# The second part of the modulation starts beside the context's products, from a spare buffer and spare PSUM banks, at low priority

## The chip, the cores and the metric

One core of one Trainium2 chip runs the whole layer in one launch. The metric is the device time of one execution in microseconds (us); lower is better. Before and after are compared by the median of several executions on the same chip.

## What is computed

One layer of a diffusion backbone over 1024 latent tokens of width 1024, with 256 context tokens. Cut to what matters:

```
mod(c)      = silu(c) @ w_mod + b_mod          # six parts of 1024: sh1 sc1 gt1 sh2 sc2 gt2
hx, hc      = rms_norm(x or ctx) * (1 + sc1) + sh1
s_f, s_b    = delta-rule states of the context (k, v, gates from hc @ w_in)
p           = hx @ w_in                        # q, k, v, z, gates, pool channels
y           = concat(delta rule(p) started from s_f, s_b ; grid pooling(p)) @ w_out
x           = x + gt1 * rms_norm(y)
x           = x + gt2 * rms_norm(conv_glu_ffn(rms_norm(x) * (1 + sc2) + sh2))
```

The modulation falls in two parts. The first (sh1 and sc1, for the latent and the context) is needed before any product with `w_in`. The second (gt1, sh2, sc2, gt2: 4096 columns of `w_mod`, 16.8 MB in float32) is needed only behind the output projection.

## The kernel before, in words

All products with large weights are made in three float32r products of a high and a low part (`hi*hi`, `lo*hi`, `hi*lo`), so every weight is split first: a rounding copy on ScalarE (ACT) and a subtraction on VectorE (DVE) or GpSimd (POOL).

The order of the work is not written out. `Streams` (lines 128 to 174) is a planner: every stage is a generator with a priority number (low goes first), and at each step the ready generator of the lowest number issues its next few instructions. What is ready when comes from `Clock` (lines 48 to 109), which keeps a planned time for each engine, a cost for each instruction and a planned landing time for each DMA. A generator yields the tiles, the named events (`"PP"`, `"X4"`, `"hX0"`) or the counted buffers (`("s", 1)`) that it waits for. All loads here are issued by `dma = SY.dma_start`, so they share SyncE's (SP's) queue. The profile's order within an engine follows this plan closely, but not to the letter.

The stages that matter here, with their priorities:

- `stream_mod` (0, line 328): the first part of the modulation, 16 loads of 512 KB. At its twelfth (`i + NW == 16`, line 355) it issues the loads of `POST` (line 34: the first context weight, latent tiles 4 to 7, four more context weights) and signals `X4`.
- `stream_xT`, `stream_h`, `stream_x1` (0 to 3): norms, transposes and the modulated `h_hi`, `h_lo` of the context and of both halves of the latent tokens ("X0", "X1"), each followed by 16 gate products (`gate_mm`, line 411, in a bank of `pc`).
- `stream_load` (3, line 546) and `stream_G` (9, line 1269): 28 jobs of large products. Jobs 0 to 7 are the context's (24 products of 256 columns each, results `pa<-c_hi,w_hi` and the like); jobs 8 to 27 are the latent's (48 products of 512 columns each, `pa<-h_hi,w_hi`). At job 8, when `hX0` and `hX1` are there, `open_gemm` (line 657) closes the pool of the loads, opens the pool `pp` and signals `PP`.
- `stream_A` (2), `stream_P` (1), `stream_Q` (0): preparation, triangular solve and scan of the delta rule, head by head. `stream_G` has the highest number, so its products fill what the others leave of TensorE (PE).
- `mod_rest` (line 1231, priority 1, spawned at line 1857): the second part of the modulation, in 32 pieces. It waits for `PP`. A piece loads two halves of 256 KB (`w_m2` in `pp`, shown as `w_m<-in_wmod`), makes eight products of 128 columns with `cs` (which the profile counts as 16, `pb<-w_m,cs`), copies the result to `mrow` on ACT, transposes it on PE (`pb<-cst,mrow`) and sums four columns on ACT (`mjk`). It has two halves of weights in all, so a piece's loads go into the buffers of the piece before. After the last piece it makes the tables `a2`, `ggd` and signals `M`, and `stream_wo(1)` takes over its buffers.
- `stream_W`, `stream_wt` and the feed-forward stages behind them, from about 580 us to the end.

PSUM has eight banks: `pa` 2, `pb` 2, `pc` 4. `slot` (line 282) hands out 4 KB buffers: before `open_dn` there are four, of which `kc`, `vc` and `gx` take three; the count `"s"` says how many are free. `cp` (line 274) is the pool of the context, closed by `open_dn`.

Of the kernel before, what the change touches and what calls it, by code (L numbers as in the profile page):

```python
# [9 lines left out]
F32 = mybir.dt.float32  # L10
# [7 lines left out]
P = 128  # L18
# [109 lines left out]
class Streams:  # L128
# [7 lines left out]
    def spawn(self, gen, prio):  # L136
        self.active.append([prio, max(self.now, self.clock.end), gen, None, 0])

    def signal(self, name):
        self.events[name] = max(self.now, self.clock.end)  # L140

    def free(self, kind, n):
        self.left[kind] = self.left.get(kind, 0) + n
        self.freed[kind] = max(self.now, self.clock.end)
# [38 lines left out]
def kernel(ctx: ExitStack, tc: tile.TileContext, I, out):  # L183
# [4 lines left out]
    streams = Streams(clock)  # L188
    spawn, signal, free = streams.spawn, streams.signal, streams.free
    dma = SY.dma_start  # L190
# [58 lines left out]
    def pb(shape):  # L249
        return psB.tile(shape, F32, name="pb", tag="pb")  # L250
# [23 lines left out]
    cp = cctx.enter_context(tc.tile_pool(name="hc", bufs=1, side="left", reuse_waits="tile"))  # L274
# [7 lines left out]
    def slot(name):  # L282

        kind = "k" if slots["k"] else "big"
        slots[kind] -= 1
        x = (da if kind == "k" else dp).tile([P, T], F32, name=name, tag=kind, bufs=NK if kind == "k" else NBIG)
        slot_of[x.name] = kind
        return x

    def free_slots(*xs):  # L290
        for x in xs:
            slots[slot_of[x.name]] += 1
        free("s", len(xs))
# [237 lines left out]
    def stream_gx():  # L531
        yield "gX0"
        yield "gX1"
        yield "Tc"
        yield from gate_tables("x", NT, gx, gtmp)
        free_slots(gx)
# [9 lines left out]
    def stream_load():  # L546
        ws = {}

        def load(i, m):
            c, h = jobs[i]  # L550
            j = h if c == "c" else {0: 4, 2: 8, 1: 0, 3: 12, 4: 16}[c] + h
            ws[i, m] = wp.tile([P, 4, P], F32, name="w_st", tag="w_st", bufs=2)
            dma(out=ws[i, m], in_=I["w_in_t"][j][:, 4 * m:4 * m + 4])

        for i in range(len(jobs)):
            his, los = [], []
            if i == 0:
                yield "w0"
            if i == 1:
                yield "X4"  # L560
                for j in range(NW):
                    if j not in wcs:
                        load_c(j)
            if i < NCJ:
                for m in range(2):
                    ws[i, m] = wcs[i][:, 4 * m:4 * m + 4]
            if i > 1:
                yield f"J{i - 2}"
            if i == NCJ - 1:
                load(NCJ, 0)  # L570
                load(NCJ, 1)
            for m in range(2):
                w = ws[i, m]
                yield (w,)
                whi = wp.tile([P, 4, P], F32R, name="w_hi", tag="w_hi")
                wlo = wp.tile([P, 4, P], F32R, name="w_lo", tag="w_lo")
                yield from split_steps(whi, wlo, w, *(SPLITS[m] if i < NCJ else (V,)))
                his.append(whi)
                los.append(wlo)
                if NCJ <= i < len(jobs) - 1:  # L580
                    load(i + 1, m)
            if i + NW < NCJ:
                load_c(i + NW)
            win[i] = his, los
            yield (whi, wlo)
            signal(f"L{i}")
        free("st0", 2)
        spawn(stream_wo(0), 5)
        spawn(mix_load(), 2)
# [637 lines left out]


    def mod_rest():
        yield "PP"  # L1230
        for j in range(32):
            ws = []
            for m in range(2):
                ws.append(pp.tile([P, 4, P], F32, name="w_m2", tag="w_m2", bufs=2))
                dma(out=ws[m], in_=I["wmod2"][j, :, 4 * m:4 * m + 4, :])
            yield tuple(ws)
            ps = pb([P, P])
            for k in range(KT):
                g = 32 * (k % 4)
                TE.matmul(ps[g:g + 32, :], lhsT=cs[:, k, :], rhs=ws[k // 4][:, k % 4, :], start=(k < 4), stop=(k >= 4),  # L1240
                          skip_group_check=True)
            yield (ps,)
            rows = pp.tile([P, P], F32, name="mrow", bufs=1)
            S.copy(rows, ps)
            yield (rows,)
            mp = pb([P, P])
            TE.transpose(mp, rows, ident)
            yield (mp,)
            jk = small.tile([P, 4], F32, name="mjk")
            S.activation(jk, mp[:, 0:P:32], AF.Copy, accum_out=mod[:, 16 + j, 0:1])  # L1250
            yield
        V.tensor_tensor(mod[:, 16:48, 0], mod[:, 16:48, 0], bm[:, 16:48], ALU.add)
        V.scalar_tensor_tensor(a2, mod[:, 32:40, 0], 1.0, sm[:, SM_GPREF:SM_GPREF + 8], ALU.add, ALU.mult)
        ggc = small.tile([P, 2, 8], F32, name="ggc")
        V.tensor_tensor(ggc[:, 0], mod[:, 16:24, 0], sm[:, SM_GPOST:SM_GPOST + 8], ALU.mult)
        V.tensor_tensor(ggc[:, 1], mod[:, 40:48, 0], sm[:, SM_GPOSTF:SM_GPOSTF + 8], ALU.mult)
        yield
        gp = pb([P, P])
        TE.transpose(gp[:16, :], ggc.rearrange("p a k -> p (a k)"), ident)
        ggs = pp.tile([P, P], F32, name="mrow", bufs=1)[:16]  # L1260
        S.copy(ggs, gp[:16, :])
        dma(out=ggd.rearrange("a k p -> (a k) p"), in_=ggs)
        yield
        signal("M")
        free("st1", 2)
        spawn(stream_wo(1), 5)
# [45 lines left out]
    def stream_wo(g):  # L1312

        pool, tag = ((wp, "w_st"), (pp, "w_m2"))[g]
        gs = slice(512 * g, 512 * g + 512)
        ks = (4, 5, 6, 7, 0, 1, 2, 3)
        ws = []

        def load():
            ws.append(pool.tile([P, 4, P], F32, name="wo_st", tag=tag, bufs=2).rearrange("p k n -> p (k n)"))  # L1320
            dma(out=ws[-1], in_=I["w_out"][ks[len(ws) - 1] * P:(ks[len(ws) - 1] + 1) * P, gs])

        for i, k in enumerate(ks):
            while len(ws) < min(i + 2, KT):
                yield f"st{g}", 1
                load()
            yield f"U{k}"
            yield (ws[i],)
            if k not in wo:
                wo[k] = [hslot(f"wo_{x}{k}") for x in "hl"]  # L1330
            yield from split_steps(wo[k][0][:, gs], wo[k][1][:, gs], ws[i])
            free(f"st{g}", 1)
            signal(f"WO{g}{k}")
        signal(f"WO{g}")
# [519 lines left out]
    spawn(stream_P(), 1)  # L1854
    spawn(stream_A(), 2)
    spawn(stream_gx(), 1)
    spawn(mod_rest(), 1)
    spawn(stream_load(), 3)
    spawn(stream_G(), 9)
    spawn(stream_wt(), 2)  # L1860
# [81 lines left out]
```

## Time and profile before

| | us |
|---|---|
| median of 3 runs | 1380.78 |
| the three runs | 1374.93, 1380.78, 1381.83 |
| the profiled execution: its own time | 1374.41 |
| its span in the profile | 1372.7 |
| PE busy in the span | 1276.5 (93%) |

The span runs from the first to the last instruction of the profile; 1.71 us lie around it. PE is TensorE's matmul stream, whose busy time counts the whole latency of a product, so that products in close order overlap. A row of the timeline gives start, duration, engine, operation, result and operands, count, and in brackets the idle time before it with what ended it. SPq is SyncE's queue of DMA issues.

### The profile page before, as it was taken

The page shows a single profiled execution, that of the slowest core. Times are in us where ns is not written, and L with a number is a line of the kernel's source. Part 1 is how long each engine was busy: PE and PEld are TensorE (multiplying, and loading weights), DVE is VectorE, ACT ScalarE, POOL GpSimd, SP SyncE. Part 2 cuts the span into 40 slices and gives each one's busy share as a digit, 9 for nine tenths or more (in the row PEclk, how much of TensorE's full clock was granted, in tenths as well). Part 3 has the DMA queues.
Part 4 walks back from the last instruction along what each step waited for, and adds up shares of the span by engine and source line. Part 5 has one row for each costly group of instructions (what it writes and reads, how often), then busy time and mean ns, then how long its engine had stood idle before and what let it go on. Part 6 is the DMA issues. An engine that isn't in the chain of part 4 may idle for free. (4 is left out here: it accounts for less than half of the span.)

```text
span 1372.7 us, 23957 instructions
## 1 busy us (share of the span) xinstructions
PE 1276.5 (93%) x8655; PEld 1003.6 (73%) x8655; DVE 999.7 (73%) x2027; ACT 624.3 (45%) x1478; POOL 333.8 (24%) x431
## 2 busy tenths in 40 slices
PE   5888999999999799988979999999999999999997
PEld 1456767777878678766767777787788887888886
DVE  1876655656788688459888998888887769655674
ACT  3555866456676345345443332332333236644540
POOL 0552434141131500012023323332333220000122
PEclk9889999999999999999999999999999999999999
DMA  9513655445462313483224465566433337976561
GB/s 344 193 41 111 204 175 146 141 131 186 120 197 70 101 58 94 151 268 136 110 74 140 166 237 210 213 230 230 154 138 123 116 122 257 308 251 197 187 212 62
DMA packets 145302, 226.55 MB, mean 165 GB/s; under 512 B 53440, under 2 KB 66592, under 8 KB 142368
## 3 DMA queue, kind: packets, MB, share of 16 engines
q1 hardware_dynamic: 144752, 224.61, 48.4%
q8 instruction: 68, 1.11, 0.3%
q14 instruction: 50, 0.41, 0.1%
q10 hardware_dynamic: 432, 0.42, 0.1%
HBM read 164.77 MB, written 60.21 MB: 164 GB/s over the span
## 5 line engine op out<-in xcount | busy, mean ns | idle before, releaser
L123 POOL TENSOR_TENSOR a<-a,a 128x512 f32<-128x512 f32 x88 | 137.9, 1568 | 354.2 <-DMA a<-in_w_up_t 130.1
L123 ACT CAST wqh<-a 128x512 fp32r<-128x512 f32 x132 | 81.1, 620 | 238.9 <-POOL a L123 62.1
L123 DVE TENSOR_TENSOR op<-dst,op 128x512 fp32r<-128x512 f32 x154 | 104.1, 717 | 62.2 <-ACT op L123 61.9
L123 PE MATMUL pa<-h_hi,w_hi 128*128 128x512 f32 x320 | 138.2, 432 | 2.5 <-ACT jk L123 1.2
L123 ACT CAST op<-dst 128x512 fp32r<-128x512 f32 x154 | 89.8, 620 | 99.1 <-PE pc L123 34.2
L123 PE MATMUL pa<-h_hi,w_lo 128*128 128x512 f32 x320 | 129.6, 405 | 1.6 <-DVE w_lo L123 1.6
L123 PE MATMUL pa<-h_lo,w_hi 128*128 128x512 f32 x320 | 130.5, 408 | 0.0
L123 PE MATMUL pc<-op 128*128 128x512 f32 x528 | 121.7, 391 | 1.3 <-DVE graw L123 1.3
L123 PEld LDWEIGHTS pc<-op 128*128 128x128 f32 x528 | 99.1, 188 | 23.2 <-DVE graw L123 1.7
L123 DVE TENSOR_TENSOR wql<-a,wqh 128x512 fp32r<-128x512 f32 x132 | 101.3, 769 | 19.0 <-ACT wqh L123 18.6
L123 DVE TENSOR_TENSOR hf<-hf 128x512 f32<-128x512 f32 x89 | 82.4, 933 | 2.2 <-DMA hf<-in_w_down 1.7
L123 POOL TENSOR_TENSOR hf<-hf,gg 128x512 f32<-128x512 f32 x16 | 21.2, 1350 | 213.7 <-ACT t L123 213.7
L123 PEld LDWEIGHTS pa<-h_hi,w_hi 128*128 128x128 f32 x320 | 61.1, 191 | 16.0 <-issue 2.8
L123 PEld LDWEIGHTS pa<-h_hi,w_lo 128*128 128x128 f32 x320 | 60.9, 190 | 13.9 <-DVE w_lo L123 1.8
L123 DVE SCALAR_TENSOR_TENSOR cv<-raw,sm,cv 128x1024 f32<-128x1024 f32 x48 | 62.3, 1297 | 11.4 <-ACT cv L123 10.9
L123 PEld LDWEIGHTS pa<-h_lo,w_hi 128*128 128x128 f32 x320 | 61.1, 191 | 9.5 <-issue 2.0
L123 DVE SCALAR_TENSOR_TENSOR hf<-graw,sm,hf 128x1024 f32<-128x1024 f32 x44 | 58.5, 1330 | 0.5
L123 PE MATMUL pa<-op 128*128 128x512 f32 x198 | 50.6, 391 | 0.0
L123 PE MATMUL pb<-op 128*128 128x512 f32 x198 | 50.4, 390 | 0.0
L123 ACT ACTIVATE ws<-pc,btg 128x128 f32<-128x128 f32 x80 | 26.9, 367 | 48.6 <-PE pc L123 48.3
L123 DVE TENSOR_TENSOR w_lo<-w_st,w_hi 128x512 fp32r<-128x512 f32 x40 | 27.6, 692 | 26.7 <-ACT w_hi L123 16.9
L123 PE MATMUL pc<-wo_h,mxh 128*128 128x512 f32 x112 | 44.4, 398 | 1.4 <-ACT mxh L123 1.4
(384 smaller groups left out, 3350.1 us busy)
## 6 DMA issues: line engine op xcount, KB each, us to landing
a<-in_w_up_t SPq DMA_DIRECT2D x90, 256.0 KB, 2.7
w_m<-in_wmod SPq DMA_DIRECT2D x64, 256.0 KB, 3.2
hf<-in_w_down SPq DMA_DIRECT2D x22, 512.0 KB, 4.2
td<-hf SPq DMA_DIRECT2D x11, 1024.0 KB, 4.5
gd<-hf SPq DMA_DIRECT2D x22, 512.0 KB, 2.8
sd<-hf SPq DMA_DIRECT2D x11, 1024.0 KB, 3.9
dst<-sd SPq DMA_DIRECT2D x44, 256.0 KB, 5.2
dst<-td SPq DMA_DIRECT2D x44, 256.0 KB, 4.8
```

The lines of the kernel that those rows point to most:

```text
L123: return f(*a, **k)
```

## The change

`mod_rest` starts at `X4` instead of `PP`, with priority 7 instead of 1. It takes the fourth 4 KB buffer (`wmk`) as its two halves of weights until `PP` is signalled, and then goes over to `w_m2` in `pp` and gives the buffer back. Until then its two PSUM tiles of a piece come from `pc` instead of `pb`, and its row of results stands in a new 512-byte tile of the context's pool. The loads of the next piece are now issued inside the piece: the first half right behind the fourth product, the second right behind the eighth; before, both were issued when the whole piece was done.

```diff
     def mod_rest():
-        yield "PP"
+        yield "X4"
+        yield "s", 1
+        wk = slot("wmk")
+        early = [wk[:, 512 * m:512 * m + 512].rearrange("p (k n) -> p k n", n=P) for m in range(2)]
+        mrow = cp.tile([P, P], F32, name="mrow0")
+
+        def load(j, m):
+
+            if j < 32:
+                first = m == 0 and "PP" not in streams.events or m == 1 and src[j, 0] is early[0]
+                src[j, m] = early[m] if first else pp.tile([P, 4, P], F32, name="w_m2", tag="w_m2", bufs=2)
+                dma(out=src[j, m], in_=I["wmod2"][j, :, 4 * m:4 * m + 4, :])
+
+        src = {}
+        load(0, 0)
+        load(0, 1)
         for j in range(32):
-            ws = []
-            for m in range(2):
-                ws.append(pp.tile([P, 4, P], F32, name="w_m2", tag="w_m2", bufs=2))
-                dma(out=ws[m], in_=I["wmod2"][j, :, 4 * m:4 * m + 4, :])
-            yield tuple(ws)
-            ps = pb([P, P])
+            ws = src[j, 0], src[j, 1]
+            if wk is not None and ws[0] is not early[0]:
+                free_slots(wk)
+                wk = None
+            pool = pb if wk is None else pc
+            yield ws
+            ps = pool([P, P])
             for k in range(KT):
                 g = 32 * (k % 4)
                 TE.matmul(ps[g:g + 32, :], lhsT=cs[:, k, :], rhs=ws[k // 4][:, k % 4, :], start=(k < 4), stop=(k >= 4),
                           skip_group_check=True)
+                if k == 3:
+                    load(j + 1, 0)
+            load(j + 1, 1)
             yield (ps,)
-            rows = pp.tile([P, P], F32, name="mrow", bufs=1)
+            rows = mrow if wk is not None else pp.tile([P, P], F32, name="mrow", bufs=1)
             S.copy(rows, ps)
             yield (rows,)
-            mp = pb([P, P])
+            mp = pool([P, P])
             TE.transpose(mp, rows, ident)
             yield (mp,)
...
-    spawn(mod_rest(), 1)
+    spawn(mod_rest(), 7)
```

## Rows read from the trace of the kernel before

**Rows 1.** Stretches: us, PE, PEld, DVE, ACT, POOL busy, PE clock, DMA share, GB/s

```profile
111.00:200.00 89.00, 80.40 (x882) 58.76 (x882) 52.03 (x138) 61.13 (x187) 25.70 (x45) 0.94 0.58 179
...
300.00:350.00 50.00, 44.14 (x737) 35.23 (x736) 32.42 (x113) 30.11 (x108) 8.83 (x22) 0.97 0.49 152
...
450.00:500.00 50.00, 40.81 (x610) 32.54 (x610) 38.24 (x119) 20.43 (x64) 19.06 (x45) 0.93 0.30 85
```

**Rows 2.** The same view, the stage of the context's products

```profile
40.00:50.00 10.00, 9.60 (x57) 5.41 (x53) 6.69 (x11) 5.25 (x12) 3.57 (x3) 0.91 0.12 47
50.00:60.00 10.00, 8.79 (x74) 4.96 (x72) 9.36 (x16) 8.13 (x19) 6.57 (x6) 1.00 0.94 368
60.00:70.00 10.00, 5.36 (x27) 2.83 (x27) 10.00 (x26) 4.64 (x10) 5.91 (x4) 0.95 0.28 96
70.00:80.00 10.00, 8.57 (x34) 5.11 (x35) 8.43 (x27) 3.70 (x11) 8.35 (x7) 0.53 0.03 11
80.00:90.00 10.00, 7.76 (x56) 6.08 (x54) 8.06 (x13) 6.27 (x11) 6.43 (x6) 1.00 0.01 2
90.00:100.00 10.00, 8.54 (x53) 3.57 (x53) 7.56 (x11) 4.67 (x8) 5.47 (x4) 1.00 0.18 62
```

**Rows 3.** Timeline of PE, from the context's products to the latent's last

```profile
70.43 1.06 PE L123 MATMUL pc<-h_hi,wg 128*32 128x512 f32 x1 [3.68 <-ACT h_hi L123]
...
87.64 0.66 PE L123 MATMUL pb<-cst,xv 128*128 128x128 f32 x4 [2.24 <-ACT h L123]
...
97.92 0.39 PE L123 MATMUL pa<-c_hi,w_hi 128*128 128x256 f32 x1
...
111.31 0.39 PE L123 MATMUL pa<-h_hi,w_hi 128*128 128x512 f32 x1
...
578.74 0.39 PE L123 MATMUL pa<-h_lo,w_hi 128*128 128x512 f32 x1
```

**Rows 4.** Groups of PE by shape, whole span: the pieces' products and transposes

```profile
L123 PE MATMUL pb<-w_m,cs 128*32 128x128 f32 x512 | 24.3, 292 | 0.0
L123 PE MATMUL pb<-cst,mrow 128*128 128x128 f32 x32 | 9.2, 288 | 2.4 <-ACT mrow L123 2.4
```

**Rows 5.** Timeline of PE: one half of a piece between two latent products

```profile
133.10 0.39 PE L123 MATMUL pa<-h_hi,w_lo 128*128 128x512 f32 x1
133.33 0.39 PE L123 MATMUL pa<-h_hi,w_hi 128*128 128x512 f32 x1
133.65 0.42 PE L123 MATMUL pb<-w_m,cs 128*32 128x128 f32 x8
134.00 0.50 PE L123 MATMUL pa<-h_lo,w_hi 128*128 128x512 f32 x1
```

**Rows 6.** Timeline of SP's queue, from the last loads of POST to pieces' loads

```profile
50.35 1.93 SPq L123 DMA_DIRECT2D w_c<-in_w_in_t  x4
...
64.41 3.54 SPq L123 DMA_DIRECT2D w_c<-in_w_in_t  x2
78.12 0.34 SPq L123 DMA_DIRECT2D gcdram<-gtmp  x1
96.92 0.82 SPq L123 DMA_DIRECT2D w_m<-in_wmod  x2
...
134.13 1.35 SPq L123 DMA_DIRECT2D w_m<-in_wmod  x2
```

**Rows 7.** What is known of tile w_m: its transfers from issue to landing

```profile
DMA to landing us min/median/max: 2.5/3.2/6.8
```

**Rows 8.** ACT's instructions of a piece: ns min/median/max, first and last start

```profile
L123 ACT COPY mrow<-pb x33: 238/265/324, 120.3 to 395.1; 128x128 f32<-128x128 f32 x32, 16x128 f32<-16x128 f32 x1
...
L123 ACT ACTIVATE mjk<-pb x32: 150/173/238, 121.6 to 391.3; 128x4 f32<-128x4 f32 x32
L123 ACT ACTIVATION_READ_ACCUMULATOR mjk<-pb x32: 192/195/275, 121.6 to 391.4; 128x1 f32 x32
```

**Rows 9.** The last scan step of the last head, on DVE's timeline

```profile
538.88 0.60 DVE L123 SCALAR_TENSOR_TENSOR X<-pc,negx,vr 128x128 f32<-128x128 f32 x2
```

## The prediction

> **What bounds the kernel now.** I read the busy time by stretches first. From 111 us, where the latent's products begin, PE is busy 90% of the time up to 200 us, 88% from 300 to 350 us and 82% from 450 to 500 us [rows 1]: `stream_G` fills whatever the delta rule leaves, so time in that stage is PE work plus some stalls. All 32 pieces of `mod_rest` lie in it, their copies from 120.3 us and their last sum at 391.4 us [rows 8]. The stage ahead of it looks different. Between 40 and 100 us PE is idle 0.40 + 1.21 + 4.64 + 1.43 + 2.24 + 1.46 = 11.4 us, while DVE is busy 76 to 100% of the slices from 50 to 100 us, and DMA hardly works from 70 us on (a share of 0.18 at most) [rows 2]. The timeline of PE says why: it stands before gate products and transposes until ACT and DVE have made the next `h`, 3.68 and 2.24 us at the longest [rows 3]; then from 97.92 us the context's products that were left behind run in close order until 111.31 us, where job 8 starts. So the end of this stage is set by the chain of `h` on ACT, DVE and POOL up to 98 us, and by PE from there. A piece put on PE before 98 us can be free; one put into 98 to 111 us only changes places.
>
> **The change part by part.**
>
> *PE work taken out of the full stage.* The products of all pieces take 24.3 us and their transposes 9.2 us [rows 4], (24.3 + 9.2) / 32 = 1.05 us a piece. A second look: two latent products start 0.67 us apart with half a piece between them [rows 5], where two neighbours without it start 0.23 us apart; that is 0.44 us for a half, 0.9 for both, and a transpose beside it. I take 1.05.
>
> *How many pieces get ahead of 98 us.* `X4` comes while SP still holds the loads of `POST`, the last of which go out from 50.35 us to 50.35 + 1.93 = 52.3 us [rows 6]. A load needs 3.2 us to land [rows 7], and its next may start once the piece's products have read the buffer, so a piece takes about 3.2 + 1.05 = 4.3 us. From 52.3 + 3.2 = 55.5 to 97.9 us that is 9.9 pieces. Against that, SP stands in order: between 52.3 and 64.4 us it waits for a context weight's buffer and from 64.41 + 3.54 = 67.95 to 78.1 us for a table on ACT [rows 6], and a load behind those waits too. The long hole from 78.5 to 96.9 us does not count, since it is the first load of `mod_rest` itself, into memory that the latent's loads still use; the new buffer has no such owner. With both other holes in the way, (42.4 - 12.1 - 10.2) / 4.3 = 4.7 pieces are left. I take 8, nearer the upper end, because the loads that land ahead of the holes need no wait; the ends are 0 and 11 (11.4 us of idle PE hold no more). Saved: 8 x 1.05 = 8.4 us, ends 0 and 11.4.
>
> *ACT.* A piece adds 0.265 + 0.173 + 0.195 = 0.63 us [rows 8], 5.1 us for eight, from 50 to 100 us, where ACT is busy 37 to 81% of a slice [rows 2] but lies on the chain of `h`. I charge two fifths to the chain, 2.0 us; the ends are 0 and 5.1. DVE and POOL get nothing. In the full stage the same 5.1 us leave ACT, at no gain, since PE sets the pace there.
>
> *DMA and SP.* Eight pieces bring 16 loads and 4.2 MB forward. Only the slice from 50 to 60 us is full, with a share of 0.94 and 368 GB/s [rows 2]; a piece's 512 KB there would hold back its neighbours 1.4 us. They are latent tiles and weights that are used later, so 0, at most 1.4. On SP the later loads now wait for PE's products in the middle of a piece; behind them stand `w_c`, `w_st`, the table's write and later the delta rule's small transfers. Before, SP also stood ready for a piece's loads and issued them as soon as its predecessor's products had started (133.65 and 134.13 us [rows 5, 6]) without a visible loss, so 0. What is late next if this fails is the last rival.
>
> *Banks, priority, memory.* `pc` has four banks, and in this stage only gate products and the first modulation use them; 0. Priority 7 is still ahead of `stream_G`'s 9. Behind 111 us the other 24 pieces come faster than before, because copy, transpose and sum now run beside the next load. That moves PE work inside the full stage without making more of it: the latent's jobs fall behind by some pieces at first and have regained it by 391 us. The new 512 bytes cost nothing in time. 0 for all of these, ends -1 and +2.
>
> *Does the gain reach the end?* The last scan step is at 538.88 us [rows 9] while latent products still run at 578.74 us [rows 3], and all that follows starts from those. PE is busy 82% from 450 to 500 us [rows 1], so some stalls there may take back part; the stalls have causes of their own and move with the rest. I keep the whole.
>
> **Sum:** -8.4 + 2.0 = -6.4 us against the profiled execution's own 1374.41 us, so 1368.0 us. That execution is 6.4 us under the median of the runs, and the four times of before scatter over 7.4 us around a mean of 1378.0. A median of after should fall where such a mean does: 1378.0 - 6.4 = 1371.6, I say 1372.
>
> **A rule that speaks against it.** PE stood once for 2.4 us before a transpose whose copy ACT had not yet made [rows 4], and all products behind it stood too. That is one of 32 pieces, in the stage where the plan and the chip agree well. By this row eight moved pieces would cost 0.6 us, which leaves -5.8 us of the sum and changes nothing; by the worst reading, each piece one such wait, they cost 8 x 2.4 = 19 us and the sum is +13 us. The second is the first rival below. The Trainium skill, "TensorE: Matmul & The Clock Gate", Part 3: Packing small matmuls, says that matmuls start and end in strict program order and only weight loads are pulled ahead of them; this row agrees.
>
> **The rivals.**
>
> *Slower: PE held by the pieces themselves.* Ahead of 98 us ACT stands up to several microseconds in order behind late `h` tiles, and the pieces' copies stand behind them on ACT; PE, in order too, then holds the transposes of X1 and the gate products that feed the same chain. A wait is worth 2.4 us [rows 4], so from the third on the net gain of 6.4 us is gone. Eight such waits give 1378 + 19 - 6 = 1391 us; five give 1384. The same can come from loads: a piece planned tightly behind its weights waits on PE for what is missing of 3.2 us. For it: the waits of 3.68 and 2.24 us show the plan off by just that much here [rows 3]. Against it: only one such wait in 32 pieces before.
>
> *Nothing at the end.* The pieces fill idle PE time, but the later stalls (PE 82% at 450 to 500 us, 88% at 300 to 350 us [rows 1]) grow by the same amount, because there the filler is short of buffers or DVE is the slow one; or the pieces come first and push context products behind 98 us, one for one. Then the time is 1378 give or take 4.
>
> *It does not do what it says.* The loads of the pieces stand in SP's queue behind the two holes [rows 6], and fewer than three pieces are made before 98 us: 1.05 x 2 = 2 us, 1376.
>
> **How the numbers follow.** Forecast 0.46, held PE 0.22, nothing at the end 0.26, not done 0.06. About 0.5%, 6.9 us, is what a measurement of this kernel can tell from no change; against the median of 1380.78 "faster" means under 1373.9 and "slower" over 1387.7. The forecast's own range is from 11.4 + 1 = 12.4 us saved to 1 us saved, 1366 to 1377: 0.38 faster, 0.08 same. Nothing at the end: 0.04, 0.20, 0.02. Held PE: 0, 0.02, 0.20. Not done: 0.06 same. Together 0.42, 0.36, 0.22. The range goes from 1361, the forecast's low end with the low runs of before (1374.4 - 12.4 = 1362), to 1390, which takes in all but the upper part of held PE.
>
> **What would show it.** Right: the first `w_m` load on SP near 52 us instead of 96.9; about eight products-and-transposes of pieces before the first latent product; that product still at 111 us or up to 2 us later; PE's idle time between 40 and 100 us down to some 4 us; the last `mjk` well before 391 us; the last latent product some 6 us earlier. Wrong: new PE waits for `mrow` or `w_m` in the list of waits; the first latent product at 115 us or later; an unchanged last latent product with longer stalls between 300 and 500 us.

## The result, and the profile after

| | before | after |
|---|---|---|
| median, 7 runs each (us) | 1380.78 | 1390.31 |
| the runs | 1374.93 to 1383.21 | 1387.18 to 1395.73 |
| ratio, 95% interval | | 1.0093 [1.0071, 1.0116] |
| span of the profiled execution | 1372.7 | 1388.6 |

The change is slower by 0.9%: 1390.31 us, where 1372 was forecast and 1390 was the upper end of the range. The profiled execution of before lies 6.4 us below the median above, so lines of the two profiles differ by more than the kernels do; executions of one kernel scatter over several us, and the ratios below, each against runs of before on the same chip, decide.

Two stretches of each kernel: from 40 us to the first latent product, and from there to the last. Columns: length, then busy time of PE, PEld, DVE, ACT and POOL (instructions), granted clock of PE, DMA share, GB/s. Before, then after; [rows 1] and [rows 2] have shorter stretches of the first.

```profile
40.00:111.31 71.31, 59.94 (x389) 39.26 (x386) 58.38 (x114) 40.84 (x83) 43.31 (x38) 0.92 0.23 86
111.31:580.33 469.02, 440.24 (x4942) 352.55 (x4941) 317.54 (x902) 267.09 (x833) 113.76 (x231) 0.97 0.45 136
```

```profile
40.00:122.05 82.05, 66.63 (x572) 44.05 (x571) 59.01 (x120) 45.64 (x116) 42.92 (x38) 0.89 0.46 153
122.05:587.95 465.90, 434.21 (x4753) 347.66 (x4751) 315.68 (x894) 257.26 (x799) 103.99 (x230) 0.97 0.42 123
```

The first latent product, at 111.31 us in [rows 3], comes at 122.05: 10.7 us later, with 11 pieces copied ahead of it. The latent stage is only 3.1 us shorter for that, although PE is busy for 6.0 us less in it: it idles 31.7 us there instead of 28.8 (length less busy time). PE's waits from 40 to 122 us in the changed kernel (total, count, longest):

```profile
PE pb L123 <- DVE rstd L123: 5.5, 1, 5.5
PE pa L123 <- ACT w_hi L123: 4.9, 1, 4.9
PE pc L123 <- ACT mrow L123: 1.5, 2, 1.0
PE pc L123 <- DMA wmk<-in_wmod: 1.2, 5, 0.4
```

The waits of [rows 3] for `h_hi` and `h` are gone; other ones of the same size stand there, and the pieces' own are small. The next place is SP's queue behind 122 us. A row is the start and the time of the issue; a group that takes longer than its count explains stood waiting. Changed kernel:

```profile
123.09 1.35 SPq L123 DMA_DIRECT2D wmk<-in_wmod  x2
124.53 0.99 SPq L123 DMA_DIRECT2D w_st<-in_w_in_t  x2
126.64 6.26 SPq L123 DMA_DIRECT2D wmk<-in_wmod  x4
133.62 0.52 SPq L123 DMA_DIRECT2D gdram<-gtmp  x1
134.19 0.58 SPq L123 DMA_DIRECT2D w_m<-in_wmod  x1
135.14 1.42 SPq L123 DMA_DIRECT2D wmk<-in_wmod  x2
136.60 0.42 SPq L123 DMA_DIRECT2D w_m<-in_wmod  x1
138.88 2.01 SPq L123 DMA_DIRECT2D wmk<-in_wmod  x2
140.94 0.42 SPq L123 DMA_DIRECT2D w_st<-in_w_in_t  x1
141.69 0.80 SPq L123 DMA_DIRECT2D w_m<-in_wmod  x2
144.28 0.33 SPq L123 DMA_DIRECT2D N<-gcdram  x1
144.66 2.73 SPq L123 DMA_DIRECT2D blk_x<-U  x4
...
166.42 3.84 SPq L123 DMA_DIRECT2D blk_i<-N  x8
```

The same transfers before:

```profile
118.74 0.53 SPq L123 DMA_DIRECT2D gdram<-gtmp  x1
...
122.66 2.58 SPq L123 DMA_DIRECT2D blk_x<-U  x4
...
126.73 0.42 SPq L123 DMA_DIRECT2D N<-gcdram  x1
...
149.29 5.15 SPq L123 DMA_DIRECT2D blk_i<-N  x8
```

Fourteen loads of pieces go out from 123 to 142 us, each where PE's products have just freed its buffer, and the first transfers of the delta rule go out among and behind them: the gates' table (`gdram<-gtmp`) 14.9 us later than before, the first `N` 17.6, the blocks for the solver (`blk_i<-N`) 17.1, all more than the 10.7 us by which this stage starts late. Not all of that is the queue. The table goes out as soon as ACT's copy of it ends, in the changed kernel and then before:

```profile
133.32 0.27 ACT L123 ACTIVATE gtmp<-pb 64x128 f32<-64x128 f32 x1
```

```profile
118.45 0.27 ACT L123 ACTIVATE gtmp<-pb 64x128 f32<-64x128 f32 x1 [1.15 <-PE pb L123]
```

And the first `N` of the changed kernel (144.28) goes out 0.06 us after PE's last products from the spare buffer:

```profile
143.79 0.43 PE L123 MATMUL pc<-wmk,cs 128*32 128x128 f32 x8
```

Whether it waited for that buffer itself or only in the queue was not tried. POOL, which starts the solver's work, waited 29.3 us ahead of its first work on `N` and 18.4 for `sR`:

```profile
149.72 1.09 POOL L123 TENSOR_SCALAR_AFFINE_SELECT N<-N 128x1024 f32<-128x1024 f32 x1 [29.29 <-DMA blk_x<-U]
...
173.34 0.63 POOL L123 COPY sB<-sR 64x256 f32<-64x256 f32 x1 [18.38 <-DMA sR<-blk_i]
```

Before, it waited 20.4 and 8.1:

```profile
131.72 1.09 POOL L123 TENSOR_SCALAR_AFFINE_SELECT N<-N 128x1024 f32<-128x1024 f32 x1 [20.41 <-DMA N<-gcdram]
...
157.00 1.37 POOL L123 COPY sB<-sR 64x256 f32<-64x256 f32 x1 [8.06 <-DMA sR<-blk_i]
```

Last, the end of the latent stage. PE in the changed kernel, from the last latent product to the first of `w_out`:

```profile
587.95 0.39 PE L123 MATMUL pa<-h_hi,w_lo 128*128 128x512 f32 x1
...
595.27 0.79 PE L123 MATMUL pa<-pmh,pwh 128*128 128x512 f32 x1 [6.94 <-ACT pmh L123]
...
606.97 0.80 PE L123 MATMUL pa<-wo_h,mxh 128*128 128x512 f32 x1 [6.15 <-ACT mxh L123]
```

That is 19.0 us, where before it was 585.92 - 580.33 = 5.6. From there the feed-forward's first product (`pa<-b11h,wqh`) is 106.7 us away, and 111.5 before, so some 9 us of these 13 stay.

### The profile page after: what moved, and what is told of

Read it like the earlier page. It is cut to its first block, busy times and chain, and to the rows that moved or that the text cites. A ratio compares the mean times of both kernels' runs of the same rounds, so it can differ in the third digit from the quotient of the medians.

```text
span 1388.6 us, 23942 instructions
## 1 busy us (share of the span) xinstructions
PE 1277.5 (92%) x8655; PEld 1003.6 (72%) x8655; DVE 1000.4 (72%) x2027; ACT 620.4 (45%) x1476; POOL 322.4 (23%) x431
## 5 line engine op out<-in xcount | busy, mean ns | idle before, releaser
L123 PE MATMUL pc<-op 128*128 128x512 f32 x528 | 121.7, 391 | 0.9 <-DVE graw L123 0.9
```

The lines of the kernel that those rows point to most:

```text
L123: return f(*a, **k)
```

## The experiments

All ratios are against the kernel before, from 4 to 12 executions of each kernel. "Late" pieces start at `PP`, "early" ones at `X4` or where noted; loads "inside" are those of the change, loads "behind" are issued when the piece before is complete. The first latent product, in us, is that of one profiled execution. In the kernel before, e10, e14 and e15 the order ahead of it is the same, and it comes at 107.8 to 112.3; differences of less than some 5 us in that column say nothing.

| run | pieces, loads | order of the rest | ratio [95%] | first latent product |
|---|---|---|---|---|
| changed kernel | early, inside | new | 1.0093 [1.0071, 1.0116] | 122.1 |
| e1_late | late, inside | new | 1.0054 [1.0034, 1.0074] | 110.2 |
| e2_prio7 | late, behind | new | 1.0095 [1.0070, 1.0120] | 107.5 |
| e3_gx0 | from `gX0`, inside | new | 1.0075 [1.0057, 1.0093] | 115.7 |
| e4_pb | early, inside, banks of `pb` | new | 1.0134 [1.0102, 1.0166] | 102.2 |
| e5_before_dve | late, behind | new | 1.0113 [1.0065, 1.0162] | 108.3 |
| e6_before_hw | late, behind | new | 1.0054 [1.0034, 1.0074] | 111.4 |
| e7_prio2 | late, behind | new | 1.0119 [1.0086, 1.0151] | 111.6 |
| e8_after_dve | early, inside | new | 1.0075 [1.0047, 1.0103] | 123.5 |
| e9_hold_change | early, inside | before's | 1.0048 [1.0031, 1.0065] | 124.9 |
| e12_hold_planner | early, inside | before's plan | 1.0045 [1.0026, 1.0064] | 125.6 |
| e10_hold_late | late, inside | before's | 1.0040 [1.0024, 1.0057] | 112.3 |
| e14_pin_late | late, inside | before's, pieces too | 1.0022 [1.0005, 1.0040] | 107.8 |
| e15_hold_before | late, behind | before's, all | 1.0002 [0.9986, 1.0019] | 109.3 |
| e11_swap | late, behind | the changed kernel's | 1.0371 [1.0340, 1.0401] | 114.6 |
| e13_hold_after | early, behind | before's | 0.9993 [0.9971, 1.0016] | 122.3 |
| e17_hold_hx0 | early, behind, products from `hX0` | before's | 1.0018 [1.0000, 1.0036] | 120.3 |
| e16_hold_gx0 | from `gX0`, behind | before's | 1.0049 [1.0034, 1.0064] | 120.7 |
| e18_after_loads | early, behind | new | 0.9992 [0.9969, 1.0014] | 121.7 |

### One part of the change at a time

```diff
 # e1_late, on the changed kernel
-        yield "X4"
-        yield "s", 1
...
+        yield "PP"
+        wk, early, mrow = None, [None, None], None
...
-                src[j, m] = early[m] if first else pp.tile([P, 4, P], F32, name="w_m2", tag="w_m2", bufs=2)
+                src[j, m] = pp.tile([P, 4, P], F32, name="w_m2", tag="w_m2", bufs=2)
 # e2_prio7, on the kernel before
-    spawn(mod_rest(), 1)
+    spawn(mod_rest(), 7)
 # e3_gx0, on the changed kernel
-        yield "X4"
+        yield "gX0"
 # e4_pb, on the changed kernel
-            pool = pb if wk is None else pc
+            pool = pb
```

With `wk` empty, e1's pieces also take their PSUM tiles from `pb`, as before the change.

> The changed kernel with its early start alone undone: the pieces wait for PP again and use pp and pb, but keep priority 7 and the loads inside the piece. Theory A (the early pieces delay the context's stage, and that delay of 10.7 us is what reaches the end): first latent product back at 111 us give or take 1, ratio to before 0.998 to 1.002. Theory B (the faster succession of pieces in the latent's stage is the cost): ratio about 1.009 as in the changed kernel. Theory C (any change of the planned order moves the end by several us): anything from 0.993 to 1.01, with the first latent product at 111 us.

> The kernel before with one number changed, mod_rest at priority 7 instead of 1. Theory A: no cost in itself, ratio 0.997 to 1.003. Theory B gives the same, since the succession of the pieces is that of before. Theory C: the order is planned anew, so the ratio may be up to 0.007 off 1 with an unchanged context stage.

> The changed kernel, but the pieces start when the gate products of X0 are issued (gX0) instead of at X4, so they cannot stand ahead of those on PE or take their bank. Theory A in its narrow form (the gate products of X0, pushed from 58 us to 74 us, are the delay): first latent product at 113 to 116 us, ratio 1.000 to 1.004. Theory A in its wide form (every piece before the first latent product costs its 1.05 us of PE there, since PE is full from 80 us on): first latent product at 118 to 122 us, ratio 1.005 to 1.009.

> The changed kernel with the early pieces' PSUM tiles from pb as before, not from pc. If the four banks of pc are the reason why the gate products of X0 come late (their bank is handed out behind those of the pieces), they are back at 58 us and the first latent product comes 3 to 6 us earlier than 122 us, ratio 1.004 to 1.007. If banks play no part, 122 us give or take 2 and ratio about 1.009; if the pieces now fight with the transposes of X1 for pb, later than 122 us.

All four lose, also the three in which the latent stage starts on time or early (e1, e2, e4: 102 to 110 us). So the late start alone isn't the cause. Of what was expected, e1 fits theory C alone; e2 lies beyond the 0.007 that theory C gave it; e3 has the first product of the narrow form and the ratio of the wide one; e4 lies outside everything. e2 is the awkward one: the kernel before with one number of its planner changed, and it loses as much as the whole change.

### Nothing but a new order

```diff
 # e5_before_dve on the kernel before, e8_after_dve on the changed one: a planned DVE instruction 2 ns longer
-            return 0.065 + n / (1920 if fast and op != "transpose" else 960)
+            return 0.067 + n / (1920 if fast and op != "transpose" else 960)
 # e6_before_hw: planned DMA issues 10 ns further apart
-            self.hw = hw + 0.45
+            self.hw = hw + 0.46
 # e7_prio2
-    spawn(mod_rest(), 1)
+    spawn(mod_rest(), 2)
```

> The kernel before with one cost in the planner changed by 2 ns (a DVE instruction's fixed part, 0.065 to 0.067 us); mod_rest and all work are as before, but the order of most instructions comes out anew. Theory C (the order of before is a good draw, and what any fresh order costs is the larger part of the loss): ratio 1.003 to 1.012, with the loss in the latent's stage. Theories A and B: nothing that they blame is touched, ratio 0.998 to 1.002.

> The kernel before with the planner's time between two DMA issues changed from 0.45 to 0.46 us; the work is unchanged, the order new. Theory C: ratio 1.003 to 1.012, but not that of the run beside it. Theories A and B: 0.998 to 1.002.

> The kernel before with mod_rest at priority 2 instead of 1. If the low number 7 is itself the loss of the run at priority 7 (pieces late, M late), 2 gives less than half of its 0.95%: ratio 1.000 to 1.004. Theory C: a number without a trend, 1.003 to 1.012 as likely at 2 as at 7.

> The changed kernel with the same 2 ns on the planner's DVE cost. Theory C: the changed kernel too is one draw, so this lies somewhere from 1.000 to 1.015 against before, off the changed kernel's 1.0093 by more than 0.002. Theory A: the first latent product stays at 120 us or later and the ratio at 1.007 to 1.011.

These change nothing that the kernel does, only what its planner believes, and through it the order of all instructions. e5, e6 and e7 cost 0.5 to 1.2%, as theory C expected; e8 lies 0.0018 from the changed kernel, within their intervals, where theory C expected more than 0.002, and in the range of theory A, so it tells nothing apart. An edit in this kernel is therefore always two edits: itself, and a new order of everything else. To read the first alone, the second has to be taken away.

### The edit with the order held

The planner's picks of the kernel before were recorded and played back, with `mod_rest`'s steps let in wherever the plan leaves PE idle ahead of `PP`, and at their recorded places behind it. As the framework orders instructions a second time, each one outside the pieces was also tied to its predecessor on its engine in the kernel before; such a tie fixes the order of issue and adds no wait.

```diff
+    def hold(self, tc):
+        for e, order in ORDERS.items():
...
+            for x, y in zip(order, order[1:]):
+                tc.add_manual_dep(mine[y], mine[x].name, mybir.DependencyInfo(mybir.DependencyClass.NoSync,
+                                  mybir.DependencyReason.DATA), reason="held order")
```

> The kernel before with its own order held in full: the same instructions in the same order on all five engines, built by the way that the other held kernels are built. Every theory: 0.998 to 1.002; what it differs from 1 is what the comparison itself can't tell.

1.0002: the method adds nothing of its own, and two equal programs compare to within 0.2%.

> The change as it is (start at X4, spare buffer, spare banks, loads inside the piece), with the order of every other instruction of all five engines held to that of the kernel before, on each engine; only the pieces are put in, 11 of them ahead of the first latent product. ORDER theory (the loss is the new order of everything else): ratio 0.994 to 1.002. PIECES theory (the pieces themselves hold PE up beside the context's products): ratio 1.006 to 1.012, first latent product at 118 to 124 us, last latent product at 587 or later. The prediction's own sum: 0.995, last latent product about 574.

> As e9_hold_change, but only the planner's order of steps is held to that of the kernel before; the second ordering, which the framework makes of the instructions, is left free. If the planner's new order is what costs: 0.994 to 1.002, as e9_hold_change. If it is the second ordering: 1.005 to 1.012, with gate products in a bunch and long waits at the last pool, as in the changed kernel.

> The pieces start at PP as before, but with the loads inside the piece (the edit of e1_late), and the order of every other instruction held to that of the kernel before. ORDER theory: 0.998 to 1.002, where the same edit with a free order gave 1.0054. LOADS theory (loads that are issued inside a piece land too late, and that is what e1_late lost): 1.004 to 1.007 and again more than 5 us of PE waiting for w_m.

e9 lies between its two theories: half of the loss stays, and the other half goes when before's order is held. e12 ties the planner's order alone and gives the same ratio, also between its theories, so holding the planner's order is enough for that. It need not lose its 0.45% as e9 does: PE idles 27.2 us in its latent stage against 31.7 in e9, and the median granted clock of its executions is 0.963 against 0.969, and 0.972 in those of before beside them. e10 shows that the first half doesn't need early pieces: with late ones and loads inside it is 0.40%. PE waited only 1.6 us for `w_m` in e10, so the loads theory was right about the price and wrong about where it is paid.

> The other way round: the pieces of the kernel before (start at PP, buffers, banks and loads as before), put into the order that the changed kernel has for every other instruction. ORDER theory: 1.006 to 1.012, as the changed kernel, though no piece is early. PIECES theory: 0.998 to 1.003.

e11 gave 1.0371 [1.0340, 1.0401], outside both. Pieces laid into an order made for others fell on the wrong places (PE waited 14.0 us for `w_m` and 6.9 for `mrow`), so this run tells nothing of the order theory.

Now the loads go back behind the piece, all else as in e9; and e14 leaves only the loads' places on SP different from the kernel before.

```diff
 # e13_hold_after, e16_hold_gx0, e17_hold_hx0; e18_after_loads with the order free
         for j in range(32):
+            if j:
+                load(j, 0)
+                load(j, 1)
...
-                if k == 3:
-                    load(j + 1, 0)
-            load(j + 1, 1)
```

> As e9_hold_change (early pieces, the order of everything else held to that of the kernel before), but both loads of a piece are issued only when the piece before it is complete, as in the kernel before. LOADS theory (what e9 and e10 lost is that loads issued inside a piece come to stand in front of the solver's transfers on SP): 0.998 to 1.002. PIECES theory (the early pieces themselves cost): 1.003 to 1.007, with the first latent product again at 118 to 126 us.

> As e10_hold_late, with the pieces' own products, copies and sums held to their places of the kernel before too: on PE, DVE, ACT and POOL nothing differs from the kernel before, only the places of the w_m loads on SP do. LOADS theory: 1.002 to 1.006, as e10_hold_late (1.004), the stores of U into blk_x and the loads of N issued 2 to 4 us later. If the pieces' own places made the loss of e10: 0.999 to 1.001.

e13 gives 0.9993: the loss is gone, and the interval doesn't meet that of e9. The pieces theory falls, at least for pieces in these places. Its two stretches, in the columns used above:

```profile
40.00:122.31 82.31, 66.62 (x557) 42.83 (x555) 60.77 (x129) 45.05 (x112) 43.26 (x38) 0.88 0.39 134
122.31:581.04 458.73, 432.23 (x4776) 347.97 (x4772) 316.01 (x888) 262.90 (x805) 111.87 (x230) 0.97 0.43 128
```

The first latent product is as late as in the changed kernel, by 11.0 us, and the latent stage is 10.3 us shorter: what the early pieces take in front they give back. e9's latent stage, with loads inside, is 4.9 us longer than that, and all of it is PE's idle time:

```profile
124.88:588.54 463.66, 431.95 (x4774) 348.60 (x4772) 313.94 (x885) 263.39 (x805) 111.23 (x230) 0.97 0.42 126
```

In the executions profiled with the order held, PE idles 26.5 us in the latent stage of e13 and 28.3 in e15 (28.8 before), with loads behind; it idles 31.7 in e9, 34.9 in e10 and 33.4 in e14, with loads inside. In front, in e13, PE stands for the first piece (waits from 40 to 124 us):

```profile
PE pc L123 <- ACT mrow L123: 9.6, 2, 7.6
PE pc L123 <- DMA wmk<-in_wmod: 4.0, 2, 3.8
```

e14 (1.0022) lies just apart from 1, though its interval meets that of e15. The solver goes through DRAM and back for every head. SP's queue at the second head in e14, then in e15, whose order is before's:

```profile
204.30 1.31 SPq L123 DMA_DIRECT2D blk_i<-N  x3
207.06 0.83 SPq L123 DMA_DIRECT2D w_m<-in_wmod  x2
207.93 3.75 SPq L123 DMA_DIRECT2D blk_i<-N  x5
212.89 0.84 SPq L123 DMA_DIRECT2D sR<-blk_i  x2
```

```profile
205.38 3.77 SPq L123 DMA_DIRECT2D blk_i<-N  x8
209.31 2.13 SPq L123 DMA_DIRECT2D sR<-blk_i  x2
```

A pair of loads has come to stand among the solver's stores, and its first load back (`sR<-blk_i`) goes out 8.6 us behind the first store instead of 3.9. Added up over the first four passes of the solver, this way takes 17.6 us before, 17.5 in e15 and 17.1 in e13, with loads behind; it takes 25.2 in e14, 26.0 in e10, 19.3 in e9, 19.9 in e12 and 19.5 in the changed kernel, with loads inside. So the held kernels with loads inside all have a longer round trip, but its length doesn't follow their losses. The waits of POOL and DVE for the solver's own transfers tell the same less clearly. From 112 to 420 us, e14 and then e13:

```profile
POOL se L123 <- DMA sc<-blk_x: 22.7, 4, 6.6
DVE st L123 <- DMA sc<-blk_x: 15.7, 3, 7.6
POOL sB L123 <- DMA sR<-blk_i: 10.7, 2, 8.8
```

```profile
POOL se L123 <- DMA sc<-blk_x: 21.5, 4, 5.9
POOL sB L123 <- DMA sR<-blk_i: 10.8, 3, 9.7
DVE st L123 <- DMA sc<-blk_x: 8.9, 2, 5.6
```

The three together are 49.1 and 41.2 us. They are 41.9 before and 39.7 in e15, with loads behind the piece, and 47.6 in e9 and 52.0 in e10, with loads inside, but only 43.5 in e12. With a free order the changed kernel has 54.5 us and e18 44.9, but e1 and e6, which lose 0.54% each, only 43.3 and 33.0; these waits don't explain every run.

### The change without its fault

> As e13_hold_after, but the pieces start behind the first half's gate products (gX0), so 11.4 us of PE waits for the first piece's load and its mrow copy are gone, and the pieces stand from 78 us on. If early pieces are worth what PE idles ahead of the latent products: first latent product at 113 to 118 us and 0.994 to 0.998. If what a piece costs there is what it gives back later: 0.998 to 1.002.

> As e13_hold_after, with the first loads issued as early as there, but the first piece's products held back until the latent operand of the first half is ready (hX0), so that PE waits neither for the load (3.8 us in e13) nor for the mrow copy (7.6 us). If early pieces are worth what PE idles: first latent product at 113 to 118 us and 0.994 to 0.998. If it comes out even: 0.998 to 1.002.

```diff
 # e17, beside the loads
         load(0, 1)
+        yield "hX0"
         for j in range(32):
```

e17 takes the 11.4 us of waits for the first piece away (2.1 for `mrow` and 1.0 for `wmk` are left), and the first latent product still comes at 120.3, not at 113 to 118; it comes out even, 1.0018, as the second of its ranges said. e16 lies outside both of its ranges: it loses 0.5% with loads behind the piece, waits of 41.9 us in the three groups above, 31.6 us of idle PE in the latent stage, and a first latent product at 120.7. Neither gains, and why e16 loses isn't known. It shows that the places of the pieces alone can cost 0.5% with the order of the rest held. As e9 and e13 differ in these places too (10 and 9 pieces are copied ahead of the first latent product, and the later ones at other times), their difference isn't proved to be the queue alone; e14 against e15, where nothing but the loads on SP differs, is 0.20%, and the intervals meet.

> The change itself, orders free as it was timed, with the one edit that both loads of a piece are issued when the piece before is complete. If the loads' places cost the changed kernel what they cost with the order held (0.5%): 1.002 to 1.006. If every new order loses its own amount whatever the edit: anywhere from 1.002 to 1.012, most likely 1.008. If the loads cost nothing in the changed kernel: 1.008 to 1.011.

e18 is the changed kernel with its loads put back, and an order of its own: 0.9992, where the change gave 1.0093. That is below all three of its ranges. SP's queue in e18, for the rows of the changed kernel above:

```profile
120.77 0.51 SPq L123 DMA_DIRECT2D gdram<-gtmp  x1
...
125.58 2.58 SPq L123 DMA_DIRECT2D blk_x<-U  x4
...
132.87 0.42 SPq L123 DMA_DIRECT2D N<-gcdram  x1
...
153.84 4.02 SPq L123 DMA_DIRECT2D blk_i<-N  x8
```

The latent stage starts at 121.7 us, as late as in the changed kernel, and the solver's blocks go out 12.6 us earlier. The wait at the end is gone too, 5.6 us from the last latent product to the first of `w_out`. This execution was the shortest of 12 (1366.11 of a median of 1373.97), so its rows are read for the order and not for the size. No run beats the kernel before by more than its interval; e13 and e18 equal it.

## Why the prediction was wrong

**What failed: "without a visible loss, so 0" for SP.** The prediction names the wait (later loads stand in the middle of a piece until PE has read the buffer) and what is queued behind it (the table's write, the delta rule's small transfers), and then prices it at 0, with no upper end. Its row [rows 5, 6] was a load that followed its predecessor's products at once (0.06 us behind their end, not as they started); it said how long SP waits for PE, not how long the solver waits for SP. With the order held, loads inside the piece measured 1.0048 where loads behind it measured 0.9993, some 7.5 us, and e10 against e15 some 5 us; PE idles 5 to 7 us longer in the latent stage of these. e14, where only the loads differ, shows the longer way through the queue, but only 0.20%, not clear of the intervals. So that this term was wrong is shown by the edit of the loads; that it is paid through the solver's transfers fits the traces, and its size by that way alone isn't shown.

**Also failed, unspoken: that the rest keeps its order.** All steps are counted against the trace of before as if only the pieces moved. A planner makes the order, yet no term and no range was given to a new one. The changed kernel loses 1.0093 - 1.0048, 0.45%, beyond what the edit loses in before's order. The 19.0 us ahead of the first product of `w_out` go with it: with the plan held they are 5.4 (e9) and 5.8 (e12). e4, e5 and e6 have 13 to 14 there too, but e2 and e7, which lose as much as the change or more, 5.7 and 4.0. That these waits are the whole of the 0.45% was not tried alone.

**"I keep the whole".** Also wrong: with both faults away the early start is worth 0.9993 and 0.9992, not 0.995. The 8.4 us saved in the latent stage are there (10.3 shorter in e13 than before, and 14.1 than in e15), but the first latent product, expected at 111 to 113, is at 120 to 122 us in all these runs. The stretch from 40 to 111 us has 11.4 us of idle time, and yet the pieces filled little of it: PE idles 15.7 us in e13 up to the first latent product and 9.8 in e17. The granted clock fell in front as well, and no term had it: from 60 to 70 and from 70 to 80 us it is 0.58 and 0.57 in the changed kernel, beside PE's waits of 4.9 and 5.5 us, near the lower of its two levels (1.2 of 2.4 GHz); [rows 2] have 0.95 and 0.53.

**Pieces.** The step asked how many come ahead of 98 us and took 8, with ends of 0 and 11. Copies on ACT ahead of 98 us are 6 in the changed kernel and 6 in e13. Another 5 and 3 come between 98 us and the first latent product, where by the prediction's own words a piece only changes places; at 1.05 us each they account for some 5 and 3 of the 11 us by which that product is late. The price of a piece holds roughly in e13, where PE's busy time in the latent stage falls by 8.0 us for 9 pieces, 0.9 each; in the changed kernel it falls by 6.0 for 11, 0.55 each.

**ACT.** Charged 2.0, at most 5.1 us. In e13 one `mrow` copy stood on ACT behind a cast that waited for DVE, and PE stood 7.6 us for it. That is the mechanism of the rival *PE held by the pieces themselves*, larger than its 2.4 us a wait, and where it is taken away (e17) nothing is gained.

**The rivals.** The time fell into the range of *PE held by the pieces* (1384 to 1391), for another reason: neither its waits for `mrow` and for the pieces' weights (2.7 us up to 122 us in the changed kernel, but 13.6 up to 124 us in e13, which loses nothing) nor its late context products are what the time was lost to. *Nothing at the end* is what the early start itself does. *It does not do what it says* is refuted by the 6 copies ahead of 98 us. Two of the signs for "right" came true and said nothing of the time: the first load of a piece goes out at 51.05 us, and the last `mjk` comes at 255.8. Of the signs named for "wrong", the waits for `mrow` and `w_m` and the first latent product behind 115 us came true, and neither was the cause; the place that tells most, the solver's transfers on SP, was not on the list.

**What stays open.** Why orders differ by up to 1.2% where nothing else does (e2, e5, e7), why before's is among the good ones, and why e18's own order is too, is not explained. The share of the loads in the changed kernel's 0.93% is 0.55% by e9 and e13; e18 alone would give 1.0%, but can't be told from a lucky order. The clock is a rival that no run took apart: the median granted clock of the executions is 0.967 in the changed kernel and 0.969 in e9, but 0.976 in e13 and 0.972 in e18 (0.971 to 0.973 in before beside these runs). A lower one can come from the longer stops of PE or be a cost of its own. By its text the planner sees no wait for a buffer that is written again under the same name, as `wmk` is, and so may place such loads too early; that was only read, not tried.

## What to carry to other kernels

- Prefetching a load into the middle of its predecessor's use puts a wait on an engine into the DMA queue, and what stands behind it waits too (8.6 us instead of 3.9 in e14). Before moving a load, list what is issued behind it, and who makes a round trip through that queue; price the wait by those, not by the load.
- Where a planner or a scheduler makes the order, time a few edits that mean nothing first, and compare an edit with the order of the rest held, or its own effect drowns: here 0.5 to 1.2% of noise against an effect of 0.5%.
- Work moved ahead of a stage gains only the idle time that it fills. In e13 nine pieces went ahead, PE's idle time there grew from 11.4 to 15.7 us, and the 10.3 us saved behind were lost in front.

## What the runs showed of the hardware

POOL's subtractions and products of the solver take 0.2 to 0.3 us, but some of before's take four times that, for the same shape:

```profile
167.68 0.27 POOL L123 TENSOR_TENSOR stmp<-sB,sX 128x48 f32<-128x48 f32 x1
168.03 1.15 POOL L123 TENSOR_TENSOR sX<-sX,stmp 128x48 f32<-128x48 f32 x1
```

DVE does these beside them:

```profile
167.68 2.67 DVE L123 SCALAR_TENSOR_TENSOR cv<-raw,sm,cv 128x1024 f32<-128x1024 f32 x2 [4.43 <-ACT cv L123]
```

POOL's slow operations follow DVE's two of 1.3 us each. The Trainium skill, "SBUF — State Buffer", Who interferes with whom, says that an instruction of DVE with two inputs in SBUF and one of GpSimd that reads SBUF contend for a pair of ports that they share, and that this pair is an exclusive lock. The slow rows agree with that; the first row, which starts together with DVE's, still takes 0.27 us. So the solver's time also hangs on what DVE happens to do beside it, which may be one way in which an order matters; no run tells how much.
